# Two layers of mixed attention on one core: ScalarE and VectorE in written order, and two output tiles prepared in the attention's end

## The chip, the cores and the metric

One core of one Trainium2 chip runs the kernel. The metric is the device time of one execution in microseconds (us). Besides TensorE (PE) the core has VectorE (DVE), ScalarE (ACT), GpSimd (POOL) and SyncE (SP), which issues the DMA transfers here. SBUF is the on-chip memory, PSUM the accumulators that TensorE writes.

## The reference

A model of two layers over 2304 tokens of width 1024 (256 context tokens, 2048 others). Each layer normalizes the tokens, projects them, mixes them in four ways, gates the results with silu and projects them back. Cut to what matters:

```python
def diff_attn_core(q, k, v, lam, lam_init, subln_g):
    s = jnp.einsum('bqhmd,bkhmd->bhmqk', q, k).astype(jnp.float32) * (DA_QK ** -0.5)
    p = jax.nn.softmax(s, axis=-1)
    w = p[:, :, 0] - lam * p[:, :, 1]
    o = jnp.einsum('bhqk,bkhd->bqhd', w.astype(v.dtype), v)
    return rms_norm(o, subln_g) * (1.0 - lam_init)
...
def gqa_core(q, k, v):
    s = jnp.einsum('bqhgd,bkhd->bhgqk', q, k).astype(jnp.float32) * (GQ_HD ** -0.5)
    p = jax.nn.softmax(s, axis=-1)
    return jnp.einsum('bhgqk,bkhd->bqhgd', p.astype(v.dtype), v)
...
    for i in range(DEPTH):
        with_ctx = i < DEPTH - 1
...
        hl = rms_norm(xl, norm_g[i]) * (1.0 + sc_l[:, None]) + sh_l[:, None]
...
         dq_l, dk_l, dv_l, dz_l, drf_l, drb_l) = split_cols(hl @ w_in[i])
...
        y_l = jnp.concatenate([ya_l * jax.nn.silu(az_l), yb_l * jax.nn.silu(bz_l),
                               yc_l * jax.nn.silu(cz_l), yd_l * jax.nn.silu(dz_l)], axis=-1)
        xl = xl + gt_l[:, None] * (y_l @ w_out[i])
...
    return rms_norm(xl, final_norm_g)
```

The products are made in three passes of a split of the weights and of the tokens into a high and a low part (`wh`, `wl`), whose sum is the full value.

## The kernel before

Each layer has four stages: two projections (`proj_attn`, `proj_cd`), `attention` and `output`. The attention runs over four rounds (one head each) of eight blocks of 256 queries against all 2304 keys, 64 full blocks over both layers; the first layer has four short context blocks besides.

A block is written out by hand in slots, 18 of them: `Slots.at(slot, fn, pr)` puts a step into a slot, `Slots.run` calls the steps by slot, then by `pr`, then as they were put in. In slots 0 to 11 lie the differential chunks (`da_chunk`: matmuls into a PSUM tile `s`, L898, then a VectorE pass that scales and finds the minimum, L903): query tile 0 in slots 0 to 5, tile 1 in 6 to 11. In 12 to 17 lie the chunks of the second attention (`g_chunk`, L937 and L942). `s` has two buffers. `da_exp` (L912, ScalarE) exponentiates a whole row in halves, once its three chunks are there. `da_comb` (VectorE) takes the second of the two attention maps from the first: three small instructions (L921 to L923), then four parts (L929); its slots are the tuple `combs`. From slot 20 on, so beside the next blocks' chunks, follow the second phase's steps: `tr(u)` transposes the combined map (L959) and copies it on ScalarE (`wt`, L963); `gs(u)` makes the second map's scores transposed (L971, L972), exponentiates them on ScalarE (`gp`, L974) and adds them up on GpSimd (`acc`, L982); three groups of `pvm` at 28.5, 34.5 and 40.5 multiply with the values (L993), which is 10.5, 16.5 and 4.5 in the slots of later blocks. `wt` and `gp` come from PSUM tiles `b`, of which there are two. `o1` copies the result (`ot`, L1000), `o2` and `o3` transpose, normalize and store it.

`pace.fill`, twice a slot, puts in matmuls of the gates (`gates`, L1158), 24 for each tile of 128 tokens and each of four groups of 256 gate columns; their weights `fw` come through an SBUF tile `fs` by `split_weights` (L124 load, L127 ScalarE copy of the high part, L128 VectorE difference). The weights of group g + 1 are loaded and split while the last tile of group g runs; there are three such renewals in each layer.

`manual_schedule({PE})` makes TensorE's instructions run in the order in which they are written; the order on the other engines, SP and GpSimd among them, is the planner's, by its own costs.

`output` is a generator that the last block calls: after the last chunk slots, `scan` of the first tile's recurrent state (with `expand_state`, L497, GpSimd), loading of `y` and `z`, eight splits of `w_out` rows through the room of `e0` and `e1`, then `mixers` (silu L1245, `pd` L1249, square L1256, rstd), `turned` (transpose L1273, L1276, L1277) and eight steps of the projection `mm3` (L139 to L141). All later tiles go through `chain(n)` and `project` after the attention's pools are closed.

## Time and profile before

| | us |
|---|---|
| median of 3 runs | 3957.22 (3955.65 to 3958.11) |
| the profiled execution | 3955.55 |
| its span | 3953.7 |
| PE busy | 3705.2 (94%) |
| DVE busy | 2669.6 (68%) |
| ACT busy | 2216.3 (56%) |
| POOL busy | 1175.1 (30%) |

The span runs from the first to the last instruction on the core; the time of an execution is 1.85 us longer. Busy time is the share of an engine that executes, over the whole span; single stretches lie above or below it. All start times below are counted in us from the span's start. The attention of the first layer lies at about 667 to 1795, that of the second at about 2637 to 3710, and each is followed by its output stage.

### The profile page before, as it was taken

How to read it: one execution, taken by the hardware profiler on the slowest of the kernel's cores; microseconds unless marked ns; L12 is line 12 of the kernel's file. 1: busy time of each engine (PE TensorE's matmuls, PEld its weight loads, DVE VectorE, ACT ScalarE, POOL GpSimd, SP SyncE). 2: the span in 40 equal slices, each digit the busy share in tenths (PEclk: the TensorE clock that was granted, in tenths of full speed). 3: DMA queues.
4: the chain of work that ended last, by engine and by line, in shares of the span. 5: the costliest groups of instructions: out<-in, count | busy, mean ns of one | idle time of the engine just before them, and what ended most of it. 6: DMA issues, size and time to landing. Idle time of an engine off the chain costs nothing.

```text
span 3953.7 us, 71741 instructions
## 1 busy us (share of the span) xinstructions
PE 3705.2 (94%) x25908; PEld 3077.9 (78%) x25908; DVE 2669.6 (68%) x6264; ACT 2216.3 (56%) x4508; POOL 1175.1 (30%) x1328
## 2 busy tenths in 40 slices
PE   7999997999998999998989999979999999999798
PEld 5888885787887887876778878867878778888576
DVE  5654443878787887866666544448877777888576
ACT  4433443666666666665544434446666666666564
POOL 1223222233333333333312222213333333333332
PEclk9999998999999999999999999989999999999899
DMA  8655334534335343326556542244343343432443
GB/s 275 195 174 176 134 140 134 155 103 133 113 103 145 105 121 101 103 90 221 182 177 203 176 147 92 83 143 123 99 137 96 116 119 96 121 99 82 146 163 121
DMA packets 407524, 537.73 MB, mean 136 GB/s; under 512 B 107832, under 2 KB 271616, under 8 KB 407168
## 3 DMA queue, kind: packets, MB, share of 16 engines
q1 hardware_dynamic: 407168, 533.14, 42.4%
q8 instruction: 205, 3.36, 0.4%
q14 instruction: 151, 1.24, 0.1%
HBM read 395.63 MB, written 137.32 MB: 135 GB/s over the span
## 4 chain that ended last, share of the span: by engine, by line
PE 75%; DVE 8%; DMA 6%; ACT 5%; issue 3%; SPq 1%; POOL 1%; DVEq 0%; ACTq 0%; POOLq 0%
PE pv L993 12%; PE pz L1158 8%; PE b L959 6%; PE s L898 5%; PE b L971 4%; PE s L937 3%; PE b L972 3%; PE po L139 2%; PE po L141 2%; PE po L140 2%; DVE e L903 2%; PE pc L139 2%; PE pc L140 2%; PE pc L141 2%; DVE e L929 1%
## 5 line engine op out<-in xcount | busy, mean ns | idle before, releaser
L982 POOL TENSOR_TENSOR acc<-acc,gp 128x512 f32<-128x512 f32 x448 | 578.6, 1292 | 955.2 <-ACT gp L974 946.9
L912 ACT ACTIVATE e<-e,dm 128x1152 f32<-128x1152 f32 x512 | 642.1, 1255 | 157.7 <-DVE e L903 155.2
L903 DVE TENSOR_SCALAR_CACHE_REDUCE e<-s,dm 128x768 f32<-128x768 f32 x512 | 515.2, 1015 | 306.9 <-PE s L898 303.2
L1158 PE MATMUL pz<-fw,fh 128*128 128x256 f32 x3264 | 710.9, 303 | 9.6 <-DMA fh<-hs 5.5
L1158 PEld LDWEIGHTS pz<-fw,fh 128*128 128x128 f32 x3264 | 528.1, 193 | 53.3 <-issue 44.9
L993 PE MATMUL pv<-wt,v 128*64 128x256 f32 x2320 | 548.3, 386 | 0.0
L993 PE MATMUL pv<-gp,v 128*64 128x256 f32 x2320 | 548.3, 386 | 0.0
L974 ACT ACTIVATE gp<-b 128x512 f32<-128x512 f32 x580 | 345.9, 596 | 359.4 <-PE b L972 344.4
L898 PE MATMUL s<-dak,daq 128*128 128x384 f32 x1568 | 420.6, 350 | 43.0 <-DMA daq<-aqk 17.9
L993 PEld LDWEIGHTS pv<-gp,v 128*64 128x64 f32 x2320 | 304.2, 138 | 173.2 <-issue 19.1
L963 ACT COPY wt<-b 128x512 f32<-128x512 f32 x580 | 340.7, 587 | 153.0 <-PE b L959 150.6
L929 DVE SCALAR_TENSOR_TENSOR e<-e,r,e 128x576 f32<-128x576 f32 x512 | 397.1, 826 | 3.4
L971 PE MATMUL b<-qa,ka 128*128 128x256 f32 x1160 | 317.1, 295 | 52.8 <-ACT gp L974 28.5
L959 PE MATMUL b<-ident,e 128*128 128x128 f32 x2304 | 354.3, 277 | 7.2 <-ACT gp L974 2.5
L993 PEld LDWEIGHTS pv<-wt,v 128*64 128x64 f32 x2320 | 304.2, 138 | 0.0
L972 PE MATMUL b<-qb,kb 128*128 128x256 f32 x1160 | 303.7, 283 | 0.0
L959 PEld LDWEIGHTS b<-ident,e 128*128 128x128 f32 x2304 | 274.2, 142 | 33.0 <-ACT gp L974 11.9
L898 PEld LDWEIGHTS s<-dak,daq 128*128 128x128 f32 x1568 | 247.1, 194 | 53.9 <-issue 19.0
L971 PEld LDWEIGHTS b<-qa,ka 128*128 128x128 f32 x1160 | 220.4, 190 | 77.7 <-ACT gp L974 37.2
L942 DVE TENSOR_SCALAR_CACHE_REDUCE junk<-s,gm 128x768 bf16<-128x768 f32 x256 | 259.7, 1015 | 29.5 <-PE s L937 15.0
L903 DVE TENSOR_SCALAR_CACHE_REDUCE e<-s 128x768 f32<-128x768 f32 x256 | 243.3, 957 | 41.7 <-PE s L898 32.8
L937 PE MATMUL s<-ka,qa 128*128 128x384 f32 (+1 forms) x784 | 216.4, 357 | 19.1 <-DMA ka<-bqk 7.5
(300 smaller groups left out, 8116.3 us busy)
## 6 DMA issues: line engine op xcount, KB each, us to landing
fh<-hs SPq DMA_DIRECT2D x272, 512.0 KB
hs<-hh SPq DMA_DIRECT2D x36, 512.0 KB
hs<-hl SPq DMA_DIRECT2D x36, 512.0 KB
hh<-hs SPq DMA_DIRECT2D x36, 512.0 KB
hl<-hs SPq DMA_DIRECT2D x36, 512.0 KB
dak<-aqk SPq DMA_DIRECT2D x96, 192.0 KB
daq<-aqk SPq DMA_DIRECT2D x136, 128.0 KB
z<-zs SPq DMA_DIRECT2D x136, 128.0 KB
```

The lines of the kernel that those rows point to most:

```text
L898: nc.tensor.matmul(s[:, u, :hc], lhsT=Q["daq"][m][:, qt * P : (qt + 1) * P], rhs=R["dak"][m][c][:, u * hc : (u + 1) * hc], start=True, sto ...
L903: nc.vector.tensor_scalar(out=E[qt, m][:, c * ch : (c + 1) * ch].rearrange("p (u f) -> p u f", u=2), in0=s[:, :, :hc], scalar1=-SC, scalar ...
L912: nc.scalar.activation(e, e, AF.Exp, bias=NM[qt, m], scale=-1.0, accum_out=L[qt][:, b, m : m + 1])
L929: nc.vector.scalar_tensor_tensor(out=E0[:, a : a + w], in0=E1[:, a : a + w], scalar=RR[qt][:, 3:4], in1=E0[:, a : a + w], op0=ALU.mult, op ...
L959: nc.tensor.transpose(s[:, j * 256 + qt * P : j * 256 + (qt + 1) * P], W[qt][:, k * P : (k + 1) * P], ident)
L963: nc.scalar.copy(WT[u], s)
L971: nc.tensor.matmul(o, lhsT=R["KA"][k // 6][:, ks], rhs=Q["QA"], start=True, stop=False)
L972: nc.tensor.matmul(o, lhsT=R["KB"][k // 6][:, ks], rhs=Q["QB"], start=False, stop=True)
L974: nc.scalar.activation(g, s, AF.Exp, scale=0.125)
L982: nc.gpsimd.tensor_tensor(out=B["acc"], in0=B["acc"], in1=g, op=ALU.add)
L993: nc.tensor.matmul(B["pv"][o : o + 64, :256], lhsT=R["V"][k // VH][:, k % VH, o : o + 64], rhs=x[:, js], start=k == 0, stop=k == nkt - 1,)
L1158: nc.tensor.matmul(ps[:, :256], lhsT=h[:, a, k % 4], rhs=w[:, b], start=k == 0 and z == 0, stop=k == KT - 1 and z == 2)
```

## The change

- `manual_schedule` now holds TensorE, ScalarE and VectorE in the order written; SP's and GpSimd's order is still the planner's.
- The first combine slots of query tile 0 go from (11, 12, 14, 16.5) to (11.5, 12.5, 14.5, 16.5); `da_exp` goes from priority -1 to 6 in its slot, so behind `tr` and `gs`; `o1` one slot later, with one buffer of `ot`; the context block's steps 2 slots later.
- `gates`: loading (`fetch`) and splitting (`split`) of a weight are steps of their own. Two loads stand ahead, and a split is followed by the load two further on. The first eight splits are put one each into slots 1.5 to 5.
- The context block's first query is loaded ahead of `ka`.
- `output` gives a list of steps with slots of the last block's end instead of eleven calls: `begin` loads the state, tile 0 and eight rows of `w_out`; then come a load of tile 1, the scan, the eight splits (VectorE alone), both tiles' gates next to each other on ScalarE, the `mixers` of tile 0 and tile 1 in steps, `turned` and eight halves of the projection. After the attention, the steps of tiles 0 and 1 go (0,0), (1,0), (0,1), (1,1).

```diff
-PE = mybir.EngineType.PE
+PE, ACT, DVE = mybir.EngineType.PE, mybir.EngineType.Activation, mybir.EngineType.DVE
...
-        self.done, self.seen, self.rest = 0, 0, 4
+        self.done, self.seen, self.rest = 0, 0, 5
...
-            cx.enter_context(self.tc.manual_schedule(engines={PE}))
+            cx.enter_context(self.tc.manual_schedule(engines={PE, ACT, DVE}))
...
-                    B["ot"] = sp.tile([P, 256], F32, name="ot", tag="ot", bufs=2)
+                    B["ot"] = sp.tile([P, 256], F32, name="ot", tag="ot", bufs=1)
...
-                s, step = (base, 1) if full else (base + 0.25, 2)
-                combs = ((11, 12, 14, 16.5), (17.5, 19, 21, 22.5))
+                s, step = (base, 1) if full else (base + 2.25, 2)
+                combs = ((11.5, 12.5, 14.5, 16.5), (17.5, 19, 21, 22.5))
...
-                            S.at(s + 1 + 2 * m + b, lambda qt=qt, m=m, b=b: da_exp(qt, m, b), -1)
+                            S.at(s + 1 + 2 * m + b, lambda qt=qt, m=m, b=b: da_exp(qt, m, b), 6)
...
-                    e = base + 24.25
+                    e = base + 26.75
...
-                S.at(e, o1, 5.5)
+                S.at(e + 1, o1, 2)
...
+            if with_ctx:
+                Qc = qload(R, 0)
...
+            for k in range(KT):
+                S.at(1.5 + 0.5 * k, pace.begin, 8)
...
-                    block(R, qload(R, 0), 0, NCTX, base)
+                    block(R, qload(R, 0) if bi else Qc, 0, NCTX, base)
...
-            S.run(base + 2)
...
-                room=[ep.tile([P, NT], F32, name=n, tag=n, bufs=b) for n, b in (("e0", 4), ("e0", 4), ("e1", 2))],
-                junk=lambda: tp.tile([P, 512], F32, name="wt", tag="wt", bufs=6),
+                room=lambda m: ep.tile([P, NT], F32, name=f"e{m}", tag=f"e{m}", bufs=4 - 2 * m),
...
-            for slot in (2, 9, 19) + tuple(20.5 + 0.5 * z for z in range(8)):
-                S.at(base + slot, lambda: next(out), 6)
+            for slot, fn in next(out):
+                S.at(base + slot, fn, 6.5)
...
-        def weight(g, k):
+        def fetch(g, k):
+            if k < KT:
+                st = raw[g, k] = fp.tile([P, 256], F32, name="fs", tag="fs", bufs=2)
+                c = (AZ, BZ, CZ, DZ)[g]
+                nc.sync.dma_start(out=st, in_=I["w_in"][i, k * P : (k + 1) * P, c : c + 256])
+        def split(g, k):
...
-            c = (AZ, BZ, CZ, DZ)[g]
-            self.split_weights(w[:, 0], w[:, 1], [I["w_in"][i, k * P : (k + 1) * P, c : c + 256]], 256, stage=(fp, "fs", 2))
+            st = raw.pop((g, k))
+            nc.scalar.copy(w[:, 0], st)
+            nc.vector.tensor_tensor(out=w[:, 1], in0=st, in1=w[:, 0].bitcast(F32), op=ALU.subtract)
+            fetch(g, k + 2)
+        raw = {}
+        for k in range(2):
+            fetch(0, k)
+            load()
...
-            weight(0, k)
-            if k in (1, 3):
-                load()
+            yield
+            split(0, k)
...
+                renew = t == tiles[-1] and g < 3
+                if renew and k == 0:
+                    for z in range(2):
+                        fetch(g + 1, z)
...
-                if t == tiles[-1] and g < 3:
-                    weight(g + 1, k)
+                if renew:
+                    split(g + 1, k)
...
-    def out_weights(self, i, W, b, gcol, stages=None):
-        for k in range(KT):
-            col = gcol[:, 0:1] if k < 2 else gcol[:, 1:2] if k >= 6 else None
-            src = self.I["w_out"][i, k * P : (k + 1) * P, b * 512 : (b + 1) * 512]
-            self.split_weights(W[0][:, k, :], W[1][:, k, :], [src], 512, col, stages and stages[k])
+    def out_rows(self, i, b, k):
+        return self.I["w_out"][i, k * P : (k + 1) * P, b * 512 : (b + 1) * 512]
...
-            def scan(t):
+            def gain(k):
+                return gcol[:, 0:1] if k < 2 else gcol[:, 1:2] if k >= 6 else None
+            def fetch(t, bst=None):
+                b0 = 128 if last and t < CTILE else 0
+                if bst is None:
+                    bst = sp.tile([P, 388], F32, name="bst", tag="bst", bufs=3 if last else 1 if front else 2)
+                nc.sync.dma_start(out=bst[:, b0:], in_=D["bst"][t, :, b0:])
+                return bst
+            def scan(t, bst=None):
...
-                bst = sp.tile([P, 388], F32, name="bst", tag="bst", bufs=1 if front else 3 if last else 2)
-                b0 = 128 if noout else 0
-                nc.sync.dma_start(out=bst[:, b0:], in_=D["bst"][t, :, b0:])
+                if bst is None:
+                    bst = fetch(t)
...
-            def load(t):
+            def load(t, room=None):
...
-                if front:
-                    y, z = front["room"][0][:, 0:DM], front["room"][0][:, DM : 2 * DM]
+                if room is not None:
+                    y, z = room[:, 0:DM], room[:, DM : 2 * DM]
...
-            def mixers(bst, B):
+            def open_gates(B):
...
+            def mixers(bst, B, sz=None):
+                y, z = B["y"], B["z"]
...
+                yield
...
-                sz = front["junk"]() if front else self.xp.tile([P, DM], F32, name="sz", tag="sz", bufs=1)
+                if sz is None:
+                    sz = self.xp.tile([P, DM], F32, name="sz", tag="sz", bufs=1)
...
+                yield
...
-                self.rstd(sp, rs[:, 1, :], rs[:, 0, :], 64, "d", sqi)
+                self.rstd(sp, rs[:, 1, :], rs[:, 0, :], 64, "d", None if front else sqi)
+                yield
...
-                bufs = 1 if front else 2
-                turn = B["turn"] = [sp.tile([P, KT, P], F32R, name=f"turn{z}", tag=f"turn{z}", bufs=bufs) for z in "hl"]
+                turn = B["turn"] = [sp.tile([P, KT, P], F32R, name=f"turn{z}", tag=f"turn{z}", bufs=2) for z in "hl"]
...
-            bsts = [scan(t) for t in order[: order.index(outs[0]) + 1]][-1:]
-            T = [load(outs[0])]
+            pre = order[: order.index(outs[0]) + 1]
+            bsts, T = [None, None], []
...
-            st = [r[:, j * 512 : (j + 1) * 512] for r in front["room"][1:] for j in range(4)]
-            self.out_weights(i, Wo[0], 0, gcol, st)
-            yield
-            mixers(bsts[0], T[0])
-            yield
-            turned(T[0])
-            yield
-            T[0]["po"] = front["bank"]()
-            for k in range(KT):
+            st = []
+            def begin():
+                bsts[:1] = [fetch(t) for t in pre]
+                T.append(load(outs[0], front["room"](0)))
+                for r in (front["room"](0), front["room"](1)):
+                    for j in range(4):
+                        st.append(r[:, j * 512 : (j + 1) * 512])
+                        nc.sync.dma_start(out=st[-1], in_=self.out_rows(i, 0, len(st) - 1))
+            def split(k):
+                wh, wl, col = Wo[0][0][:, k, :], Wo[0][1][:, k, :], gain(k)
+                nc.vector.tensor_scalar(out=wh, in0=st[k], scalar1=1.0 if col is None else col, scalar2=None, op0=ALU.mult)
+                if col is None:
+                    nc.vector.tensor_tensor(out=wl, in0=st[k], in1=wh.bitcast(F32), op=ALU.subtract)
+                else:
+                    nc.vector.scalar_tensor_tensor(
+                        out=wl, in0=st[k], scalar=col, in1=wh.bitcast(F32), op0=ALU.mult, op1=ALU.subtract
+                    )
+            def scan_first():
+                bsts[:] = [scan(t, b) for t, b in zip(pre, bsts)][-1:] + [None]
+            def second_state():
+                bsts[1] = fetch(outs[1], st[1][:, 0:388])
+            def half(k):
+                if k == 0:
+                    T[0]["po"] = front["bank"]()
...
-                yield
+            M = {}
+            def mix(n):
+                if n not in M:
+                    M[n] = mixers(bsts[n], T[n], st[0])
+                next(M[n], None)
+            plan = [(2, begin), (4.9, lambda: T.append(load(outs[1], front["room"](1)))), (6, scan_first)]
+            plan += [(7 + z, lambda k=k: split(k)) for k, z in enumerate((1, 2, 3.3, 4.3, 5.3, 6.3, 7.3, 8.3))]
+            plan += [(10, lambda: mix(0)), (10.2, lambda: open_gates(T[0])), (10.3, lambda: open_gates(T[1])), (10.4, self.table)]
+            plan += [(11, lambda: mix(0)), (12, lambda: mix(0)), (11.5, second_state), (14, lambda: mix(0))]
+            plan += [(13.5, lambda: scan(outs[1], bsts[1])), (17, lambda: mix(1)), (18, lambda: mix(1)), (19, lambda: mix(1))]
+            plan += [(17.5, lambda: turned(T[0])), (20.5, lambda: mix(1)), (22.8, lambda: turned(T[1]))]
+            plan += [(z, lambda k=k: half(k)) for k, z in enumerate((19.5, 20, 20.5, 21, 21.5, 22, 23, 23.5))]
+            yield plan
...
-            T.append(load(outs[1]))
-            bsts.append(scan(outs[1]))
+            T.append(load(outs[2]))
+            bsts.append(scan(outs[2]))
...
-            self.out_weights(i, Wo[1], 1, gcol)
+            for k in range(KT):
+                self.split_weights(Wo[1][0][:, k, :], Wo[1][1][:, k, :], [self.out_rows(i, 1, k)], 512, gain(k))
...
-                    mixers(bsts[n], T[n])
+                    open_gates(T[n])
+                    for _ in mixers(bsts[n], T[n]):
+                        pass
...
-            steps = [(n, b) for n in range(NO - tail) for b in range(2)]
+            steps = [(0, 0), (1, 0), (0, 1), (1, 1)] + [(n, b) for n in range(2, NO - tail) for b in range(2)]
...
-            chain(1)
...
-                if n == 1 and b == 0:
-                    turned(T[1])
-                elif n and k + 1 < len(steps) and steps[k + 1][1] == 0:
+                if n > 1 - b and k + 1 < len(steps) and steps[k + 1][1] == 0:
...
-                if b == 0:
-                    chain(n + 2)
+                if b == 0 and n:
+                    chain(n + 1 if n == 1 else n + 2)
+                elif n == 1:
+                    chain(3)
...
```

## Rows read from the trace of the kernel before

**Rows 1.** Windows, two blocks: length, busy us of each engine, clock, DMA share, GB/s.

```profile
2752.58:2783.78 31.20, 30.46 (x240) 26.02 (x238) 25.07 (x55) 21.26 (x38) 11.03 (x9) 1.00 0.30 96
842.00:873.90 31.90, 31.57 (x247) 27.06 (x249) 25.68 (x52) 21.70 (x40) 11.58 (x10) 1.00 0.35 110
```

**Rows 2.** TensorE's waits, 2700 to 3660: total us, times, longest.

```profile
PE b L971 <- ACT wt L963: 20.5, 29, 0.7
```

**Rows 3.** Timeline of VectorE, 2783.7 to 2798: start, us, engine, line, operation, count.

```profile
2783.78 2.27 DVE L929 SCALAR_TENSOR_TENSOR e<-e,r,e 128x576 f32<-128x576 f32 x3
2787.09 1.02 DVE L903 TENSOR_SCALAR_CACHE_REDUCE e<-s,dm 128x768 f32<-128x768 f32 x1 [1.04 <-PE s L898]
...
2788.03 0.95 DVE L942 TENSOR_SCALAR_CACHE_REDUCE junk<-s 128x768 bf16<-128x768 f32 x1
...
2792.28 0.16 DVE L921 TENSOR_TENSOR l<-l 128x2 f32<-128x2 f32 x1
...
2793.63 0.38 DVE L923 SCALAR_TENSOR_TENSOR r<-l,nlam,r 128x1 f32<-128x1 f32 x1
2794.04 3.00 DVE L929 SCALAR_TENSOR_TENSOR e<-e,r,e 128x576 f32<-128x576 f32 x4
```

**Rows 4.** Timeline of TensorE, 2786.4 to 2793.2.

```profile
2786.53 0.52 PE L898 MATMUL s<-dak,daq 128*128 128x384 f32 x2
...
2789.46 0.52 PE L937 MATMUL s<-ka,qa 128*128 128x384 f32 x2
...
2791.66 0.51 PE L937 MATMUL s<-ka,qa 128*128 128x384 f32 x2
...
2793.07 0.43 PE L993 MATMUL pv<-gp,v 128*64 128x256 f32 x1
```

**Rows 5.** Timeline of VectorE, 2664 to 2673, where combines and chunks alternate.

```profile
2667.76 0.82 DVE L929 SCALAR_TENSOR_TENSOR e<-e,r,e 128x576 f32<-128x576 f32 x1
2668.49 1.01 DVE L942 TENSOR_SCALAR_CACHE_REDUCE junk<-s,gm 128x768 bf16<-128x768 f32 x1
...
2669.42 0.81 DVE L929 SCALAR_TENSOR_TENSOR e<-e,r,e 128x576 f32<-128x576 f32 x1
```

**Rows 6.** Timeline of TensorE, 2667.8 to 2673; in brackets idle before, and its releaser.

```profile
2669.56 0.61 PE L937 MATMUL s<-ka,qa 128*128 128x384 f32 x2 [0.70 <-DVE junk L942]
```

**Rows 7.** Timeline of VectorE, 2680.2 to 2682.2.

```profile
2680.33 1.82 DVE L929 SCALAR_TENSOR_TENSOR e<-e,r,e 128x576 f32<-128x576 f32 x1
```

**Rows 8.** Timeline of GpSimd, 2680.2 to 2682.2.

```profile
2680.24 1.29 POOL L980 TENSOR_TENSOR acc<-gp 128x512 f32<-128x512 f32 x1 [51.29 <-ACT gp L974]
```

**Rows 9.** Timeline of GpSimd, 2783 to 2797.

```profile
2787.53 1.29 POOL L982 TENSOR_TENSOR acc<-acc,gp 128x512 f32<-128x512 f32 x1 [4.10 <-ACT gp L974]
2790.50 1.29 POOL L982 TENSOR_TENSOR acc<-acc,gp 128x512 f32<-128x512 f32 x1 [1.68 <-ACT gp L974]
2792.71 1.27 POOL L982 TENSOR_TENSOR acc<-acc,gp 128x512 f32<-128x512 f32 x1 [0.92 <-ACT gp L974]
```

**Rows 10.** Chain that ended last, longest pieces: start, us, what.

```profile
3145.96 8.15 DMA fs<-in_w_in_dram
...
3408.47 5.44 DMA fs<-in_w_in_dram
```

**Rows 11.** Timeline of TensorE, 938 to 950.

```profile
946.93 0.38 PE L971 MATMUL b<-qa,ka 128*128 128x256 f32 x1 [3.84 <-ACT gp L974]
```

**Rows 12.** TensorE's waits, 660 to 720: total us, times, longest.

```profile
PE s L898 <- DMA daq<-aqk: 17.9, 2, 17.4
```

**Rows 13.** Windows around the two tails, columns as in the first group.

```profile
1748.00:1832.00 84.00, 65.77 (x366) 47.07 (x365) 44.51 (x111) 49.35 (x76) 34.05 (x47) 0.84 0.53 173
3660.00:3760.00 100.00, 71.56 (x415) 50.51 (x414) 54.78 (x133) 55.44 (x86) 37.07 (x52) 0.83 0.44 144
```

**Rows 14.** TensorE's waits, 1748 to 1832 and 3660 to 3760.

```profile
PE pd L1249 <- POOL SXb L497: 5.7, 2, 2.9
...
PE pd L1249 <- POOL SXb L497: 13.3, 2, 8.2
```

## The prediction

> **What bounds the kernel now.** I read the share of each engine first, then the stages, then single blocks. TensorE is the engine that runs nearly all the time, so I looked for what it does in one block of the attention, the unit of which there are 64 (32 in each layer). A block of the second layer lasts 31.20 us, and TensorE is busy for 30.46 of it; one of the first layer lasts 31.90 with 31.57 busy, while VectorE is at 25.07 and 25.68 and ScalarE at about 21.5 [rows 1]. So a steady block is bound by TensorE's order, and only something that makes TensorE wait can change it. The list of waits shows what is left: in the second layer one wait of 0.7 us in nearly every block, for the copy `wt`; 20.5 us in all [rows 2]. Elsewhere TensorE loses time in three places: at the start of the attention, at the six renewals of the gate weights, and in the two tails, where one stage goes over into the next.
>
> **Part 1: ScalarE and VectorE in the order emitted.** What I need is where a block's VectorE work lies, because a chunk of scores has only two PSUM tiles (`s`): a chunk's matmuls wait until VectorE has reduced the chunk two before it.
>
> Before, the planner put three of the four first combines (L929, query tile 0) into the shadow of a group of pv matmuls, ahead of the last differential chunk, and the four of tile 1 into the next such shadow [rows 3]. The five g chunks between them (g12 to g16) meet no combine. I name chunks by their slot: da11 is the last differential one, g12 to g17 are the six of L937. TensorE's distances from da11 (2786.53) are 2.93 to g14, 5.13 to g16 and 6.54 to the next pv group [rows 4].
>
> After, the queue follows the slots: da11, combine 0 with its three small instructions, g12, combine 1, g13, g14, combine 2, g15, g16, combine 3. The shadow of the pv group before da11 stays empty on VectorE. Working it through with the rows: VectorE starts da11 0.56 after its matmul (2786.53 to 2787.09) and takes 0.94 [rows 3, 4], so it ends at 1.50. The small instructions are two of 0.16 and one of up to 0.38 [rows 3], with their starts about 0.8 (estimate): 2.30. Combine 0.73, chunk 0.93, as where the two alternate [rows 5]: combine 0 ends at 3.03, g12 at 3.91 to 3.96, combine 1 at 4.67, g13 at 5.55, g14 at 6.48. TensorE follows 0.14 after the end of the chunk (2669.42 to 2669.56), and that stretch shows the very pattern, chunk and combine in turn, with TensorE waiting 0.70 per chunk [rows 5, 6]. So g14 can't start before 4.05 to 4.10, instead of 2.93, and g16 not before 6.6, instead of 5.13: **1.5 us later per block**, with nothing behind it to give it back, since everything on TensorE follows in order. That is the lower end.
>
> The upper end comes from GpSimd. A combine that starts while GpSimd adds `acc` waits for it: at 2680.33 one took 1.82 us, against 0.81 and 0.82 elsewhere [rows 5], where an addition of 1.29 had begun at 2680.24 [rows 7, 8]; the small L923 that took 0.38 ended at 2794.01, just behind the addition that ended at 2793.98 [rows 3, 9]. In the present order the combines hardly meet an addition. In the new one they lie right among them: additions start 1.0 and 3.97 after da11 [rows 9]. The first holds the small instructions from 1.50 to 2.28, so that combine 0 ends near 3.65; the second, starting then, holds combine 1 until 4.95; g14 ends at 7.45, and g16 starts 2.5 us late. The Trainium skill has this as a rule (SBUF — State Buffer, "SBUF: two separate sides"): a VectorE instruction with two inputs in SBUF and a GpSimd instruction that reads SBUF exclude each other for a whole instruction. It speaks against this part of the change; the trace agrees with it, by the 1.82 [rows 7, 8]. I take the middle of 1.5 and 2.5, **2.0**, as the additions themselves move with the delays.
>
> In slots 0 to 5 the combines of tile 1 now alternate with the differential chunks as well. There the chunks stand further apart on TensorE, so the bounds are 0 and 1.5 (two combines and an addition of 1.29 [rows 7, 8] less 0.6 to 1.4 of slack, estimates); I take 0.4. Against that, `wt` no longer stands behind an exponential in the queue (its priority goes from ahead to behind): the 0.7 is 20.5 us in one layer [rows 2], 0.3 a block over both. **Per block 2.0 + 0.4 − 0.3 = 2.1; times 64 = +134 us** (ends: 1.2 and 3.7, that is +77 and +237).
>
> **Part 2: gate weights in two steps.** At a renewal the chain of the end now goes once through a load of `fs`, 5.44 to 8.15 us from issue to landing (six such places) [rows 10], and TensorE loses 3.84 in the one that I followed, waiting for `gp`, which stands behind the blocked copy on ScalarE [rows 11]; with the lower clock just behind it 4 to 7 us each (estimate). After, the first two loads go out a few us before their split, but each further one only behind the split two before it. Splits come every 24 gate matmuls / 8, which at two gate tiles a block is 31.2 / 16 = 1.95 us; two of them give a load 3.9 us, and it needs 5.44 to 8.15. So there are three waits of 1.5 to 4 us, now on ScalarE and VectorE both, since both follow the emission: 5 to 12 in the sum, less what the two spare `b` tiles take up. I take 2.5 us more at each: **+15** for six, with ends of −30 (all of the present loss saved) and +45 (+7.5 each). The Trainium skill gives a fit for one transfer (DMA: Bandwidth & Descriptors, "Anatomy of one DMA — SWDGE (gpsimd) path"), 2.0 us and the bytes at 436 GB/s; 128 KB would take 2.3 us by it, an estimate for another issuing path than SP's, and then no renewal would wait. The trace shows two to four times that [rows 10].
>
> **Part 3: the start.** The context's query goes ahead of `ka` on SP's queue, so that the 17.4 us wait for `daq` in the first layer [rows 12] shrinks; the eight first splits are spread over slots 1.5 to 5, and each pair is again tied to a load of 5.44 or more [rows 10], in the same queues as the first chunks' reductions. A gain of up to 12 and a loss of up to 15 (three loads, less what lies beside the loads of `dak`) are both possible: **0**. The context block's slots moved by 2 and the later `ot` with one buffer have VectorE and ScalarE work of under 1 us each and nothing late behind them: 0, and no more than 1 us per layer if the cover is gone.
>
> **Part 4: the tails.** TensorE is busy 65.77 of 84 us around the first tail and 71.56 of 100 around the second, at clocks of 0.84 and 0.83 [rows 13]. Waits of `pd` for the expanded state are 5.7 and 13.3 us in them [rows 14]. With two tiles prepared and eight loads of `w_out` ahead, one `pd` wait goes in each, and the splits, now two VectorE instructions each, lie in the last block's second half. New: `open_gates` of tile 1 stands on ScalarE ahead of the last `wt` copies and waits for tile 1's load, behind about 3 MB on the queue. I take **−10 each, −20** (ends −40: both waits and the clock behind them; +10: the new wait is the longer).
>
> **Sum.** The profiled execution took 3955.55 us, its span 3953.7 and 1.85 around it; the median of the runs is 1.7 higher, which is within the rounding here. 3955.55 + 134 + 15 + 0 − 20 = 4085.
>
> **The rivals.**
> A. *The emitted order costs TensorE nothing*, because the combines slip past the chunks in time, or the queue isn't the one I read off the slots. For it: VectorE has 6 us free in a block [rows 1]. Against: the two PSUM tiles, and the 0.70 waits where the pattern exists already [rows 6]. Then 3955.55 − 20 (tails) + 15 − 16 (`wt`) = 3935, with smooth renewals 3890. It ends on the other side: the point is g16's matmuls starting less than about 0.2 us late per block; at 0.3 x 64 = 19 the gains are used up.
> B. *Renewals without waits*, the stall as forecast: 3955.55 + 134 − 30 − 20 = 4040. For it: two loads are out early; against: 5.44 us at the least [rows 10].
> C. *The lock decides* (each combine meets an addition): 3955.55 + 3.7 x 64 + 15 − 20 = 4187.
> D. *Small stall, gains equal to it*: 3950 to 3965, no change.
>
> **Chances.** Forecast (4020 to 4160, B's time in it) 0.68; A 0.20; C beyond 4160 0.06; D 0.06. The range reaches from A's middle, 3925, to 4160 and leaves out about half of A's chance and C. Differences under 0.2% (8 us) can't be told from no change: faster 0.20, same 0.06, slower 0.74.
>
> **What would show it.** Right: blocks of 33 to 34 us in both layers; TensorE waiting for `junk` at the chunks of L937, twice a block and 1 us or more each, some 100 us in all; VectorE idle for about 3 us ahead of da11; combines of 1.1 to 1.8 us beside `acc`; the 0.7 waits for `wt` gone; three waits of ScalarE for `fs` in each renewal; fewer `pd` waits in the tails. Wrong: blocks still at 31.2 (rival A), or longer blocks in which TensorE waits for `gp` or `wt` and not for VectorE, which would mean that ScalarE's order, not VectorE's, is the cost.

## The result and the profile after

| | before | after |
|---|---|---|
| median, us | 3956.43 (4 runs) | 4247.86 (4 runs, 4243.61 to 4251.12) |
| ratio, 95% interval | | 1.0734 (1.0717 to 1.0751) |
| profiled execution, its span | 3955.55, 3953.7 | 4243.61, 4241.8 |

The change costs 291 us. The forecast was 4085, so +128: the right direction, by the mechanism named, and less than half the size; 4248 lies above the range and above rival C.

The block of the second layer that stood for the steady state [rows 1] is now 35.39 us long. Windows, columns as there:

```profile
2926.93:2962.32 35.39, 31.76 (x238) 26.34 (x237) 26.45 (x51) 20.66 (x39) 10.89 (x10) 1.00 0.26 85
```

TensorE issues nearly the same instructions (238 against 240) in 4.19 us more: 2.9 of them are idle, and 1.3 are counted as busy time (31.76 instead of 30.46). Its waits from 2900 to 3940, longest two of the list:

```profile
PE s L937 <- DVE junk L942: 59.5, 56, 1.5
PE s L898 <- DVE e L903: 23.3, 29, 0.9
```

Before, neither chunk waited for VectorE in a steady block; the wait for `wt` [rows 2] was the largest. The same stretch as in [rows 4], from da11 on, TensorE:

```profile
2953.30 0.51 PE L898 MATMUL s<-dak,daq 128*128 128x384 f32 x2
...
2957.85 0.62 PE L937 MATMUL s<-ka,qa 128*128 128x384 f32 x2 [1.48 <-DVE junk L942]
...
2959.78 0.63 PE L937 MATMUL s<-ka,qa 128*128 128x384 f32 x2 [0.63 <-DVE junk L942]
...
2961.07 0.52 PE L937 MATMUL s<-ka,qa 128*128 128x384 f32 x2
...
2962.32 0.43 PE L993 MATMUL pv<-gp,v 128*64 128x256 f32 x1
```

g14 starts 4.55 after da11, g16 7.77 and the pv group 9.02, instead of 2.93, 5.13 and 6.54 [rows 4]. VectorE and GpSimd in it, which answer to [rows 3] and [rows 9]:

```profile
2953.85 1.02 DVE L903 TENSOR_SCALAR_CACHE_REDUCE e<-s,dm 128x768 f32<-128x768 f32 x1 [3.09 <-PE s L898]
...
2954.79 0.82 DVE L921 TENSOR_TENSOR l<-l 128x2 f32<-128x2 f32 x1
...
2956.10 0.82 DVE L929 SCALAR_TENSOR_TENSOR e<-e,r,e 128x576 f32<-128x576 f32 x1
2956.84 0.95 DVE L942 TENSOR_SCALAR_CACHE_REDUCE junk<-s 128x768 bf16<-128x768 f32 x1
...
2957.71 1.14 DVE L929 SCALAR_TENSOR_TENSOR e<-e,r,e 128x576 f32<-128x576 f32 x1
2958.78 0.94 DVE L942 TENSOR_SCALAR_CACHE_REDUCE junk<-s 128x768 bf16<-128x768 f32 x1
```

```profile
2954.30 1.29 POOL L982 TENSOR_TENSOR acc<-acc,gp 128x512 f32<-128x512 f32 x1 [3.94 <-ACT gp L974]
2956.97 1.27 POOL L982 TENSOR_TENSOR acc<-acc,gp 128x512 f32<-128x512 f32 x1 [1.38 <-ACT gp L974]
```

The sum of `l` (L921), 128 x 2 elements and 0.16 us before, starts behind da11 and ends at 2955.61, just behind the addition that ends at 2955.59. The held sum and the first combine delay g12's reduction; the second, 1.14 us long, ends 0.61 behind the second addition's end at 2958.24. The pv group of slot 10.5 has an empty VectorE beside it (3.09 us idle, in the first row).

The other half of the loss lies behind the pv group of slot 16.5, with the combines of tile 1:

```profile
2931.93 1.74 DVE L929 SCALAR_TENSOR_TENSOR e<-e,r,e 128x576 f32<-128x576 f32 x1
2933.59 0.94 DVE L903 TENSOR_SCALAR_CACHE_REDUCE e<-s 128x768 f32<-128x768 f32 x1
...
2934.46 1.50 DVE L929 SCALAR_TENSOR_TENSOR e<-e,r,e 128x576 f32<-128x576 f32 x1
2935.88 0.95 DVE L903 TENSOR_SCALAR_CACHE_REDUCE e<-s 128x768 f32<-128x768 f32 x1
```

```profile
2931.73 1.32 POOL L982 TENSOR_TENSOR acc<-acc,gp 128x512 f32<-128x512 f32 x1 [4.41 <-ACT gp L974]
2934.06 1.28 POOL L982 TENSOR_TENSOR acc<-acc,gp 128x512 f32<-128x512 f32 x1 [1.01 <-ACT gp L974]
```

```profile
2936.89 0.61 PE L898 MATMUL s<-dak,daq 128*128 128x384 f32 x2 [0.84 <-DVE e L903]
```

Two combines of 1.74 and 1.50 us, each of them caught by an addition, stand ahead of two differential chunks, and TensorE's third chunk waits 0.84 for the second of these chunks. This part lost 1.76 us. With 0.23 for `zs` the idle time of TensorE in it is 1.07; the other 0.7 is counted as busy time (10.70 instead of 10.02 us for the same matmuls), and why is not shown. The transposes (L959) of the first combine's result start at 2933.97, 0.3 behind its end.

The three pv groups of a block are marks that cut it into three parts. Their distances in us (median of the blocks of the second layer, from the starts of the groups' first matmuls) in every kernel of this study (the changed ones are explained under The experiments), and beside them what lies outside the steady blocks: from the last projection's end to the first pv group of layer 0; what a block with a renewal costs above the median (layer 1, three renewals); from the last pv group to the end.

| kernel | time | 10.5 to 16.5 | 16.5 to 4.5 | 4.5 to 10.5 | start | renewals | tail |
|---|---|---|---|---|---|---|---|
| before | 3956 | 10.10 | 10.02 | 11.08 | 72.0 | 7.5, 12.9, 4.8 | 241.2 |
| after | 4248 | 12.47 | 11.78 | 11.15 | 86.0 | 8.6, 10.0, 4.9 | 231.1 |
| only_pe | 3958 | 9.97 | 10.05 | 11.32 | 81.8 | 5.2, 12.5, 5.4 | 232.4 |
| only_act | 4099 | 11.54 | 10.81 | 11.15 | 81.9 | 9.9, 15.0, 8.6 | 230.5 |
| only_dve | 4226 | 13.08 | 11.29 | 10.91 | 85.8 | 7.8, 10.6, 6.0 | 232.1 |
| few_adds | 4084 | 11.46 | 10.53 | 11.16 | 85.0 | 10.3, 13.6, 6.7 | 232.9 |
| few_adds_before | 3945 | 10.10 | 10.02 | 11.08 | 70.0 | 6.5, 13.8, 5.0 | 240.7 |
| old_slots | 4084 | 10.07 | 11.78 | 11.16 | 85.2 | 9.9, 17.1, 7.0 | 230.7 |
| shadow_slots | 4473 | 13.75 | 15.25 | 11.15 | 89.4 | 9.5, 8.7, 5.9 | 231.4 |
| exps_early | 4253 | 13.82 | 11.77 | 11.15 | 90.4 | 7.3, 9.7, 3.2 | 231.0 |
| own_places | 4058 | 9.81 | 10.55 | 11.15 | 97.6 | 16.9, 24.0, 13.9 | 231.9 |
| act_exps | 4029 | 10.22 | 10.56 | 11.15 | 87.7 | 11.0, 14.2, 7.8 | 230.7 |
| deep_pe | 3917 | 9.97 | 10.05 | 11.32 | 69.9 | 1.3, 7.7, 1.3 | 230.3 |
| deep_places | 3986 | 9.81 | 10.55 | 11.15 | 92.5 | 7.8, 14.6, 7.4 | 231.4 |

From before to after the steady block of layer 1 grows by 2.37 + 1.76 + 0.07 = 4.20; in layer 0 the median goes from 31.62 to 35.99, 4.37. Over 32 blocks each that is 274 of the 288 us by which the span grew. The starts add 14.0 and 9.2, the renewals of layer 1 about −2, the tails (from the last pv group on) −5.2 and −10.1; some 8 us I leave unassigned. Medians hide that a block has two lengths: in the second layer 9 of the 31 distances from one pv group of slot 10.5 to the next, away from the renewals, are 36.7 to 37.0 instead of 35.4.

### The profile page after: what moved, and what is told of

Read it like the earlier page. It is cut to its first block, busy times and chain, and to the rows that moved or that the text cites. A ratio compares the mean times of both kernels' runs of the same rounds, so it can differ in the third digit from the quotient of the medians.

```text
span 4241.8 us, 71855 instructions
## 1 busy us (share of the span) xinstructions
PE 3809.5 (90%) x25908; PEld 3129.6 (74%) x25908; DVE 2782.0 (66%) x6280; ACT 2181.2 (51%) x4474; POOL 1197.0 (28%) x1328
## 3 DMA queue, kind: packets, MB, share of 16 engines
q14 instruction: 152, 1.25, 0.1%
## 4 chain that ended last, share of the span: by engine, by line
PE 64%; DVE 17%; DMA 7%; issue 5%; ACT 4%; SPq 1%; POOL 1%; ACTq 0%; DVEq 0%; POOLq 0%
PE pv L993 12%; PE pz L1175 6%; PE s L898 5%; DVE e L903 4%; DVE junk L942 4%; PE b L959 3%; DVE e L929 3%; PE s L937 3%; PE b L971 2%; DMA fs<-in_w_in_dram 2%; PE po L139 2%; PE b L972 2%; PE po L141 2%; PE po L140 2%; PE pc L139 2%
## 5 line engine op out<-in xcount | busy, mean ns | idle before, releaser
L1175 PE MATMUL pz<-fw,fh 128*128 128x256 f32 x3264 | 731.4, 310 | 23.3 <-ACT zs L1182 20.4
L1175 PEld LDWEIGHTS pz<-fw,fh 128*128 128x128 f32 x3264 | 542.7, 198 | 93.1 <-issue 48.5
L929 DVE SCALAR_TENSOR_TENSOR e<-e,r,e 128x576 f32<-128x576 f32 x512 | 523.1, 1022 | 4.5
L898 PE MATMUL s<-dak,daq 128*128 128x384 f32 (+1 forms) x1568 | 427.1, 354 | 104.6 <-DVE e L903 74.1
L937 PE MATMUL s<-ka,qa 128*128 128x384 f32 (+1 forms) x784 | 244.4, 395 | 154.2 <-DVE junk L942 148.0
L959 PE MATMUL b<-ident,e 128*128 128x128 f32 x2304 | 365.4, 282 | 19.0 <-DVE e L929 7.4
L971 PE MATMUL b<-qa,ka 128*128 128x256 f32 x1160 | 320.4, 297 | 20.5 <-ACT wt L963 13.3
L959 PEld LDWEIGHTS b<-ident,e 128*128 128x128 f32 x2304 | 285.4, 145 | 45.9 <-ACT gp L974 13.2
L972 PE MATMUL b<-qb,kb 128*128 128x256 f32 x1160 | 312.3, 290 | 0.0
L937 PEld LDWEIGHTS s<-ka,qa 128*128 128x128 f32 x784 | 129.5, 205 | 209.6 <-DVE junk L942 175.9
```

What stands on the lines that cost most here:

```text
L898: nc.tensor.matmul(s[:, u, :hc], lhsT=Q["daq"][m][:, qt * P : (qt + 1) * P], rhs=R["dak"][m][c][:, u * hc : (u + 1) * hc], start=True, sto ...
L929: nc.vector.scalar_tensor_tensor(out=E0[:, a : a + w], in0=E1[:, a : a + w], scalar=RR[qt][:, 3:4], in1=E0[:, a : a + w], op0=ALU.mult, op ...
L937: nc.tensor.matmul(s[:, u, :hc], lhsT=Q["QA"][:, qt * P : (qt + 1) * P], rhs=R["KA"][c][:, u * hc : (u + 1) * hc], start=True, stop=True,)
L959: nc.tensor.transpose(s[:, j * 256 + qt * P : j * 256 + (qt + 1) * P], W[qt][:, k * P : (k + 1) * P], ident)
L971: nc.tensor.matmul(o, lhsT=R["KA"][k // 6][:, ks], rhs=Q["QA"], start=True, stop=False)
L972: nc.tensor.matmul(o, lhsT=R["KB"][k // 6][:, ks], rhs=Q["QB"], start=False, stop=True)
```

## The experiments

**Whose order is it?** The change with `manual_schedule` holding fewer engines.

```diff
-            cx.enter_context(self.tc.manual_schedule(engines={PE, ACT, DVE}))
+            cx.enter_context(self.tc.manual_schedule(engines={PE}))        # only_pe
+            cx.enter_context(self.tc.manual_schedule(engines={PE, ACT}))   # only_act
+            cx.enter_context(self.tc.manual_schedule(engines={PE, DVE}))   # only_dve
```

> All of the change, but only TensorE's order is as written; the planner orders ScalarE and VectorE again. Theory 1 (the order of VectorE costs the steady blocks 4.2 us each, 64 x 4.2 = 269 of the 291 us): blocks back at 31.2 to 31.9 us and a time of 3957 + 291 - 269 = about 3980, or less where the serial loads of the first splits come out of the queues, 3955. Rival 2 (the other edits, tails, gates and start, cost most of it): above 4150, with blocks that stay over 34 us.

Measured: 3957.52, ratio to before 1.0003 (0.9993 to 1.0012). The other edits together are neutral, so the whole loss needs the written order of the two engines; the moved slots, for one, count only where that order is held. In this neutral sum the tails gain 8.0 and 8.8 us, the starts lose 9.8 and 4.0, and the blocks, 31.34 us instead of 31.20 in the second layer, lose a little.

> All of the change, with TensorE and ScalarE as written and VectorE by the planner. Theory 1 (VectorE's written order is the cost): no more than 30 us over the run with TensorE alone written (3957), so 3950 to 3990, blocks under 32 us. Rival 3 (ScalarE's order takes a large part, as its late exponentials did in the run with the combines in the shadows): 4050 to 4150.

> All of the change, with TensorE and VectorE as written and ScalarE by the planner. Theory 1: the whole loss is there, 4200 to 4260, blocks of 34.5 to 36 us. Rival 3 (ScalarE's order): 4000 to 4100.

Measured: 4099.22 and 4226.30. The second is as theory 1 has it. The first is not: 142 us by ScalarE alone, where theory 1 allowed 30. The rival had part of the truth. The two don't add (142 + 269 against 291). What ScalarE's order does in only_act is seen on VectorE, waits from 2900 to 3600 of only_act:

```profile
DVE l L921 <- ACT e L912: 47.9, 40, 2.1
```

The planner, which orders VectorE here by its own costs, seems to have put a combine where it expected the exponentials to be done; in the written order VectorE waits up to 2.1 us for them, and the chunks queue behind the waiting combine. In after itself VectorE's list of waits from 2900 to 3940 has no exponential in it, and leaving ScalarE to the planner there saves only 22 us (4248 to 4226): with both orders held it is VectorE's that costs.

**Order or exclusion?** GpSimd's additions left out but for the first.

```diff
-                    elif u > 1:
-                        nc.gpsimd.tensor_tensor(out=B["acc"], in0=B["acc"], in1=g, op=ALU.add)
-                    if u == nu - 1:
+                    if u == min(1, nu - 1):
```

> Leaves out all but the first of GpSimd's eight acc additions in each block, and the add of the halves (a sum plus one stands for it), so the second attention's denominators are not the reference's; all else is the changed kernel. Theory 1a (the exclusion of a two-input VectorE instruction and a GpSimd addition is the larger half of the stall): the combines fall from a mean of 1.02 us to 0.81, blocks go from 35.4 to 32.7 us, that is -2.7 x 64 = -170, time about 4080. Rival 1b (the order alone, one combine after each chunk, costs the 4.2): blocks stay at 35 us, time 4230 to 4250.

> The kernel before without all but the first of GpSimd's acc additions of a block, and a sum plus one in place of the add of the halves; the denominators are not the reference's. It says what the additions cost where the planner orders VectorE. Theory 1a (there they hardly meet a combine; 24 of 520 in the trace of before): 3945 to 3957. Rival (the additions cost the old order as much, so that the run with few additions in the changed kernel shows nothing on the exclusion): under 3850.

Measured: 4083.81 and 3945.40. In the changed kernel the additions cost 164 us, in the kernel before 12 (0.9971, 0.9960 to 0.9982). The costliest groups show it, the combine's line in after and in few_adds (mean ns in the last but one field):

```profile
L929 DVE SCALAR_TENSOR_TENSOR e<-e,r,e 128x576 f32<-128x576 f32 x512 | 523.1, 1022 | 4.5
```

```profile
L929 DVE SCALAR_TENSOR_TENSOR e<-e,r,e 128x576 f32<-128x576 f32 x512 | 419.8, 821 | 4.5
```

Of the 512 full combines 160 take over 0.95 us in after, 13 in before and 3 in few_adds. What is left without the exclusion, 11.46 − 10.10 = 1.36 and 10.53 − 10.02 = 0.51 per block, is the price of the order alone (the first addition of a block is still there); the additions bring 1.01 and 1.25 more. They do it through VectorE: the lists of waits of TensorE, ScalarE and VectorE in after, 2900 to 3940, name no wait for GpSimd. In after, 191 combines start inside an addition; they end 0.61 us behind it (median), however early they began, and the 56 sums L921 that do so end 0.02 behind it. By the Trainium skill's rule (SBUF — State Buffer, "SBUF: two separate sides") the two exclude each other for a whole instruction; the runs agree with these 0.61 and 0.02, also for an instruction of two elements a partition (0.82 instead of 0.16).

**Which combines?** The first slots as before.

```diff
-                combs = ((11.5, 12.5, 14.5, 16.5), (17.5, 19, 21, 22.5))
+                combs = ((11, 12, 14, 16.5), (17.5, 19, 21, 22.5))      # old_slots
```

> Combines of tile 0 at the slots of before (11, 12, 14, 16.5), so that the first is written ahead of da11; the rest is the changed kernel. Theory 1: one combine with its small instructions lies in the pv shadow, two instead of three delay g16; blocks of 33 to 34 us, time 4248 - 64 x 1.9 = about 4125. Rival 3 (ScalarE's order): no difference, 4240 to 4250.

Measured: 4084.04. The first part of the block is back at 10.07, the second stays at 11.78: the half slot, which puts the first combine behind da11 instead of ahead of it, costs 2.4 us a block in the second layer and 2.9 in the first (blocks of 33.0 and 33.1 us are left), 164 us in all. I had expected 1.9 a block. In this order as many combines are caught by an addition as in after (162 and 160 over 0.95 us), 27 of the 32 fourth combines of tile 0 in the second layer among them, and yet its first part loses nothing: TensorE waits for `junk` for 1.0 us in all from 2850 to 3750. So the number of meetings is not the cost: a meeting costs where TensorE waits for a chunk behind it.

**Places.** A square of exponentials and combines, late or at the planner's places.

```diff
+                exps = ((4.6, 4.7, 7, 8), (10.62, 10.72, 13, 15))                        # exps_early
-                            S.at(s + 1 + 2 * m + b, lambda qt=qt, m=m, b=b: da_exp(qt, m, b), 6)
+                            S.at(base + exps[qt][2 * m + b] if full else s + 1 + 2 * m + b, lambda qt=qt, m=m, b=b: da_exp(qt, m, b), 6)
-                combs = ((11.5, 12.5, 14.5, 16.5), (17.5, 19, 21, 22.5))
+                combs = ((10.6, 10.7, 10.8, 10.9), (16.6, 16.7, 16.8, 16.9))             # shadow_slots
+                combs = ((10.6, 10.7, 10.8, 16.5), (16.6, 16.7, 16.8, 16.9))             # own_places, with exps
```

> All three engines as written, with the four combines of tile 0 put right behind the pv group at slot 10.5 (10.6 to 10.9) and those of tile 1 right behind that at 16.5 (16.6 to 16.9), where the planner had them. Theory 1 (combines among the chunks, and GpSimd's additions that hold them there): blocks of 31.2 to 31.6 us, waits of TensorE for junk under 0.3 us, time 4248 - 64 x 4 = about 3990. Rival 3 (ScalarE's written order, its exponentials behind tr and gs, is the cost): blocks stay above 34 us, time above 4150.

Measured: 4472.86, the slowest of all, where I expected 3990. VectorE, waits from 3000 to 4000, and two places of its timeline:

```profile
DVE l L921 <- ACT e L912: 86.6, 44, 3.0
```

```profile
3053.34 0.16 DVE L921 TENSOR_TENSOR l<-l 128x2 f32<-128x2 f32 x1 [1.15 <-ACT e L912]
...
3053.99 4.02 DVE L929 SCALAR_TENSOR_TENSOR e<-e,r,e 128x576 f32<-128x576 f32 x4
...
3068.20 0.16 DVE L921 TENSOR_TENSOR l<-l 128x2 f32<-128x2 f32 x1 [2.69 <-ACT e L912]
...
3068.86 4.04 DVE L929 SCALAR_TENSOR_TENSOR e<-e,r,e 128x576 f32<-128x576 f32 x4
```

The last half exponential is written in slot 10 or 16, where ScalarE is behind with `wt` and `gp`; it ends 1.15 and 2.69 us after VectorE has got to the combine. In an order that is held, four combines and all chunks behind them wait with it. The planner's combines could stand in the shadows only because its exponentials were early, too; the next two runs test that.

> The changed kernel with only the exponentials at the planner's places (4.6, 4.7, 7, 8 and 10.62, 10.72, 13, 15); the combines stay among the chunks. With the shadow run (combines moved alone, 4473) and the run with both moved (4058) it makes the square of four. Theory 5 (two things must both be right: a combine among the chunks stalls them, and a combine ahead of a late exponential stalls them more): 4180 to 4250, blocks of 34 to 35.5 us. Rival (late exponentials were the whole cost): 4050 to 4080.

> All three engines as written, with the exponentials and combines at the places that the planner gave them: exponentials of tile 0 at 4.6, 4.7, 7 and 8, of tile 1 at 10.62, 10.72, 13 and 15; combines of tile 0 at 10.6, 10.7, 10.8 and 16.5, of tile 1 at 16.6 to 16.9. Theory 1 with what the shadow run showed (a combine must not be written ahead of a late exponential, nor among the chunks): blocks of 31.2 to 31.8 us, time 3950 to 3995. Rival 4 (an order held by hand costs the block something by itself, whatever the places): blocks over 33 us, time over 4070.

Measured: 4253.07 and 4057.92. Early exponentials alone give nothing (4180 to 4250 was expected). (The first part's median of 13.82 instead of 12.47 is no new loss: this part takes either about 12.45 or about 13.9 us in both kernels, and the median falls on the other of the two.) Both together bring the block to 31.51 us, as expected, but the time misses its 3950 to 3995. The square is not exact: the last combine of tile 0 stands at 10.9 in shadow_slots and at 16.5 in own_places. Theory 5 holds for the planner's places: combines there need the exponentials there. It does not hold for the first part in general, which old_slots brought back to 10.07 with late exponentials, by its first combine alone. The time is still 100 us over before, and the table says where most of that is: renewals of 13.9 to 24.0 us instead of 4.8 to 12.9, and starts of 97.6 instead of 72.0. In after the stalls probably hid the renewals' part.

> TensorE and ScalarE as written, VectorE by the planner, and the exponentials at the planner's places. Theory 5 (the 142 us that ScalarE's order cost alone came from exponentials that end late and hold the planner's combine on VectorE): blocks from 33.5 to 31.3 to 31.7 us, time 3960 to 4040, the rest being the gate weights' loads on ScalarE. Rival (the copies' order behind tr and gs costs it): still about 4100.

Measured: 4029.33, blocks of 31.92 us; VectorE's wait for ScalarE's exponentials falls from 47.9 to 6.0 us (700 us of the second layer each). So about half of what ScalarE's order cost, 70 of 142 us, was the late exponentials. Of the 72 us left over only_pe some 47 are still in the steady blocks (31.92 and 32.71 us in the two layers, second first, instead of 31.34 and 31.83), 11 in the starts and the rest mostly at the renewals; what holds the blocks is not shown.

**The loads.** Four deep, and a group's first four issued within the tile before.

```diff
-                st = raw[g, k] = fp.tile([P, 256], F32, name="fs", tag="fs", bufs=2)
+                st = raw[g, k] = fp.tile([P, 256], F32, name="fs", tag="fs", bufs=4)
-            fetch(g, k + 2)
+            fetch(g, k + 4)
-                if renew and k == 0:
-                    for z in range(2):
+                if t == tiles[-2] and g < 3 and k == 4:
+                    for z in range(4):
                         fetch(g + 1, z)
```

with `range(4)` for the first group's loads as well.

> The change with TensorE's order alone as written, and the gate weights' loads four deep, the first four of a group issued within the tile before. Theory 6 (the loads' round trip of 5 to 8 us is what a renewal costs): 3957 less 4 to 6 us at each of six renewals and some at the two starts: 3915 to 3940, under the kernel before. Rival (the waits are hidden by other work or TensorE loses it to the clock anyway): 3950 to 3960.

> All three engines as written with exponentials and combines at the planner's places (4058), and the gate weights' loads four deep, early. Theory 6: what is left of the loss there is the renewals (13.9 to 24 us each against 5 to 13 before) and the starts, where both engines wait in their order for a load: 3960 to 3990. Rival 4 (the written order itself): 4040 to 4060.

Measured: 3917.43, ratio to before 0.9898 (0.9884 to 0.9911), and 3985.52, ratio 1.0075 (1.0062 to 1.0088). The first is faster than both kernels: by 37 us than the kernel before measured beside it (3954.78) and by 330 than after. Both came out in the range expected. Against only_pe, the renewals of the second layer fall from 5.2, 12.5 and 5.4 us to 1.3, 7.7 and 1.3, and the starts by 11.9 and 7.5. The list of ScalarE's waits from 2650 to 3620 of deep_pe has no `fs` any more; in own_places, from 2750 to 3750, it has:

```profile
ACT fw L1152 <- DMA fs<-in_w_in_dram: 28.2, 12, 4.7
```

## Why the prediction was half right

**The stall at g14 and g16: the mechanism right, the term too small.** By hand, without the exclusion, g14 could start 4.05 and g16 6.6 us after da11. In few_adds they start at 3.89 and 6.78 and the part grows by 1.36 (forecast 1.5). With the exclusion the hand working said 2.5; measured are 2.64 at g16 and 2.37 at the pv group. The failing step is the choice of the middle, 2.0, "as the additions themselves move with the delays". They did move, and still caught a combine of tile 0 in 28 of the 32 blocks of the second layer; the likely reason, which no run tests, is that both hang on the same chain, as `gs` is written beside the chunk that the combine follows. There was some luck in the 2.5: the working has the second addition end at 4.95, where [rows 9] have it from 3.97 to 5.26 behind da11; in after it ran from 3.67 to 4.94.

**Tile 1's combines: the step that failed most.** I took 0.4 from bounds of 0 and 1.5 and measured 1.76. The order alone is 0.51, near my value; the other 1.25 came with the additions, so it is again the exclusion. I had applied it to tile 0 step by step and to tile 1 only as an end of a range that I then didn't weigh. One combine of 1.74 us, the like of that in [rows 7], takes 0.93 longer than a free one of 0.81; that alone is more than the whole term.

**`wt`: a gain that did not come.** I credited 0.3 a block for a copy that no longer stands behind an exponential. The part that holds it (4.5 to 10.5) went from 11.08 to 11.15. Its wait shrank (0.4 instead of 0.7) and didn't go, and TensorE's busy time in that part rose by as much (10.71 instead of 10.35, medians); why is not shown.

Together: 2.37 + 1.76 + 0.07 = 4.20 instead of 2.1, times 64 = 269 instead of 134. That is 135 of the 163 us by which the forecast fell short (291 less 128); the starts are 23 more.

**The starts: forecast 0, measured +14.0 and +9.2.** Together that is 23.2, more than the +15 that I allowed. The place was named, loads in pairs in the chunks' own queue. ScalarE's waits in the first start, 660 to 760 of after:

```profile
ACT fw L1151 <- DMA fs<-in_w_in_dram: 40.8, 6, 23.3
```

and TensorE's, in which the 17.4 us for `daq` [rows 12] is gone, a wait of 15.1 for `dak` stands in its place, and one for VectorE comes on top:

```profile
PE s L898 <- DVE e L903: 18.4, 5, 12.6
PE s L898 <- DMA dak<-aqk: 16.2, 3, 15.1
```

I had set the gain of the earlier `daq` against the loads, as if the two were apart. The gain mostly didn't come, as the next load in the queue was waited for instead; and the `fs` load behind the 23.3 us was issued only at 694.50, behind `dak`, `ka`, `daq` and `qa`, and took 6.30 more. Four-deep loads shorten the first start by 11.9 us where TensorE's order alone is held (81.8 to 69.9 from only_pe to deep_pe) and by 5.1 where all three are (97.6 to 92.5).

**The renewals: +15 forecast, about −2 measured in layer 1**, but, as it seems, for a reason that I didn't see: TensorE's stalls gave the loads time. With the stalls removed (own_places) a renewal costs 9.1 to 11.1 us more than before, above my upper end of 7.5. A term taken from the old block's pace is only right if the block keeps that pace. By the Trainium skill's fit for another issuing path (DMA: Bandwidth & Descriptors, "Anatomy of one DMA — SWDGE (gpsimd) path") such a load would take 2.3 us, an estimate. That is met by two loads in the first start of after (2.49 us from 701.71 and 2.51 from 706.39) and not at the renewals, where [rows 10] have 5.44 to 8.15.

**The tails: −20 forecast; −5.2 and −10.1 measured**, in only_pe −8.0 and −8.8. Right in size for the second, half for the first, but the sign named for it failed in the first: TensorE's waits for the expanded state (L1275 in after) are

```profile
PE pd L1275 <- POOL SXb L497: 5.7, 3, 4.5
...
PE s L1275 <- POOL SXb L497: 1.5, 1, 1.5
```

from 1860 to 2000, 7.2 us instead of 5.7 [rows 14], and from 3960 to 4060 they are 13.6 instead of 18.8 (13.3 [rows 14] and one of 5.5 in a tile `s`). What shortened the first tail was not looked into.

**The rivals.** A fell: g16 is 2.6 us late, not under 0.2; the combines do not slip past the chunks in time. B's condition came nearest in deep_pe, where ScalarE no longer waits for `fs`; two renewals of the second layer still cost 1.3 us there and one 7.7. C, "each combine meets an addition", was nearest, and I gave it 0.06. It should have had more: the step by step working with the rows had led to its value for tile 0.

**What I looked for.** Blocks came to 35.4 and not 33 to 34; the waits for `junk` were twice a block and 59.5 us in one layer, as said; VectorE idle for 3.09 us ahead of da11, as said; combines of 1.1 to 1.8 us beside `acc`, as said, and these should have been in the sum. The waits for `wt` are not gone (0.4), and the waits for the expanded state in the first tail are not fewer.

## What to carry to other kernels

When an engine's order is to be held by hand, first write down where the planner had put each step, and work through one steady block with durations, two-buffer rules and the additions of the engine next to it; if that working gives a value, take it and not the middle between it and a milder one. Move a consumer and what it waits for together: combines in the shadows with late exponentials were the slowest kernel of all, and with both at the planner's places (one combine of the eight moved besides) the kernel was 415 us faster. Half a slot can be the whole matter: the first combine behind a chunk instead of ahead of it cost 164 us. A split that sits in an engine's held order must have its load issued well ahead, or the load's round trip is paid in that engine's queue.

## What the runs showed of the hardware

VectorE's instructions with two inputs in SBUF waited for a GpSimd addition at both sizes seen: L921, on 128 x 2 elements, took 0.82 us instead of 0.16, and a combine that starts inside an addition ends 0.61 us behind that addition's end (2958.24 to 2958.85; the median of 191). GpSimd waited likewise: in the block shown its add of halves took 1.12 us beside a combine of 1.50, where such an add takes 0.73 elsewhere (at 1752.61 in the kernel before). The additions cost 12 us in the kernel before and 164 in after. With the first combine ahead of da11 (old_slots) as many combines were caught and the time was 164 us shorter, so where a caught instruction stands decides what it costs. A 128 KB load of `fs` took from 2.49 us (701.71, first start of after) to 8.74 (2965.32, a renewal of own_places) from issue to landing.
